# Scores and outputs of a retention head placed between the groups of the large products that follow its projections

## The chip, the cores and the metric

The kernel runs on one core of one Trainium2 chip. The metric is the device time of one execution in microseconds (us), less is better. Engine names in the profile: PE is TensorE (PEld its weight loads), DVE is VectorE, ACT is ScalarE, POOL is GpSimd, SP is SyncE.

## The reference

One decoder layer with two head groups that read the same projected input: 16 RWKV-7 heads of 64 and 4 RetNet heads of 256, for 256 tokens of width 2048. The outputs of both are concatenated and go through one output projection, then a layer norm, an MLP of width 8192 and a second norm. The change is in the RetNet part. Cut down:

```python
def _retention_mix(q, k, v, g, gn_w):
    ...
    q = _rotary(q, cos, sin)
    k = _rotary(k, cos, sin) * RET_HEAD ** -0.5
    ...
    scores = jnp.einsum('bhncd,bhnmd->bhncm', qc, kc) * decay_mask[:, None]
    intra = jnp.einsum('bhncm,bhnme->bhnce', scores, vc)
    ...   # plus the state carried over from the chunk before
    y = _head_norm(y, RET_GN_EPS) * gn_w.reshape(RET_HEADS, RET_HEAD)
    return y.reshape(B, T, D_RET) * jax.nn.silu(g.astype(jnp.float32))
```

Since 256 tokens are two chunks of 128, the kernel computes each head as one masked product over all 256 tokens: the decay between any two tokens is in a mask.

## The kernel before

All weights come as a stream of 202 chunks of 128 x 2048. Each chunk is loaded in two halves into `raw` (three buffers); ScalarE rounds a half to `whi` (L136) and VectorE subtracts for the rest `wlo` (L138), four buffers each. Every large product is three products: high by high, high by low, low by high. A chunk is used in one of two ways. `stat_tile` (L141) keeps the weights as the stationary operand: 48 products of 128x256 at L154. `mov_chunk` (L159) moves them: 24 products of 128x512 at L170. Both yield four times per chunk.

Up to about 480 us the generator `large` issues the input projections of the RWKV units and of the heads. The four RWKV units (each with four heads) are generators of their own with hundreds of small steps: a decay product (L530, L562), a triangular solve on VectorE (`prod` L677, `xb` L680) whose result comes back by DMA and is multiplied at L726, a scan over chunks (L758 to L792, with `rhs` and `sa` copied by ScalarE at L763 and L768), and a norm whose result is written to `mxh` and `mxl` (L816, L817). `interleave` advances each live unit by one step per yield of `large`. A yield of "end" advances no unit; it only counts towards RET_SPLIT, which says after how many of them the next unit's input projections come. The order written out this way is then the input of a scheduler, which may move instructions on each engine.

`retention` (L397) runs twice, for two heads each. It first forms v for both heads (`vt`), four moved chunks. Then for each head and for q and k in turn it issues two `stat_tile`, VectorE multiplies the bank by cosine and sine (`ra` L417, `rb` L419) and GpSimd subtracts and adds the halves into `qk` (L422, L423). After two bare yields come the scores: four products (L434, L436) into a small bank `sc` of a ring of four, two multiplications with the mask by VectorE (`pm`, L439, L440); then "end", and the outputs: three products (L445 to L447), statistics, an inverse root on VectorE and the norm into `vt` (L458). After both heads the gate follows: four moved chunks, a tanh, products with `vt`, and transposes of `gth` at L473.

Of the kernel before, what the change touches and what calls it, by code (L numbers as in the profile page):

```python
# [17 lines left out]
P = 128  # L18
T = 256
# [57 lines left out]
WO_LAST = 58 + 12  # L77

LAG = dict(lora=2, scan=3, sq=5, rn=1, kk=7, bt=2, g1=1, btok=1, ktok=2, g2=1, sub=3, xt=2, vtok=8, bg=4, d1=3, d2=1, f1=1, sa=2, st=2, yc=2)

SUB_YIELD = (6, 10, 13, 16, 19, 21, 23, 25, 27, 29)
NSHORT = 10
# [18 lines left out]
def tile_hybrid_layer(ctx, tc, xT, xtok, ws, pp, lup, glup, ln1r, ln2r, cst, rope, dmask, eye, out):  # L101
# [169 lines left out]
    with ExitStack() as rctx:  # L271
# [124 lines left out]

        def retention():  # L397

            for n in range(2):

                vt = rp.tile([P, 1024], F32, name="vt", tag="vt", bufs=1).rearrange("q (a n) -> q a n", a=2)
                banks = [mm_bank(), mm_bank()]
                for kq in range(4):
                    yield from mov_chunk(tok_act(xh, xl, kq), banks, kq == 0, kq == 3)
                    if kq == 3:
                        for tt in range(2):
                            S.copy(vt[:, tt], banks[tt])
                    yield "end"
                for h in (2 * n, 2 * n + 1):
                    qk = []  # L410
                    for w in range(2):
                        bank = mm_bank()
                        yield from stat_tile(xact, bank[:, hs[0]])
                        yield "end"
                        yield from stat_tile(xact, bank[:, hs[1]])
                        ra, rb_ = tmp("ra"), tmp("rb")
                        V.tensor_tensor(out=ra, in0=bank, in1=ropet, op=ALU.mult)  # L417
                        for i in range(2):
                            V.tensor_tensor(out=rb_[:, hs[i]], in0=bank[:, hs[i]], in1=ropet[:, hs[1 - i]],  # L419
                                            op=ALU.mult)  # L420
                        o = tmp("qk%d" % w)
                        G.tensor_tensor(out=o[:, hs[0]], in0=ra[:, hs[0]], in1=ra[:, hs[1]], op=ALU.subtract)  # L422
                        G.tensor_tensor(out=o[:, hs[1]], in0=rb_[:, hs[0]], in1=rb_[:, hs[1]], op=ALU.add)  # L423
                        qk.append(o)
                        if w == 0:
                            yield "end"
                    q, k = qk
                    yield
                    yield
                    sc = sm_bank()  # L430
                    dmt = rp.tile([P, T], F32, name="dmt", tag="dmt", bufs=2)
                    nc.gpsimd.dma_start(out=dmt, in_=dmask[:, T * h:T * h + T])
                    for i in range(2):
                        TE.matmul(sc[:, 0:T], k[:, T * i:T * i + P], q[:, hs[i]], start=i == 0, stop=i == 1)  # L434
                    for i in range(2):
                        TE.matmul(sc[:, T:T + P], k[:, T * i + P:T * i + T], q[:, T * i + P:T * i + T],  # L436
                                  start=i == 0, stop=i == 1)
                    pm = tmp("pm", n=384)
                    V.tensor_tensor(out=pm[:, 0:T], in0=sc[:, 0:T], in1=dmt, op=ALU.mult)  # L439
                    V.tensor_tensor(out=pm[:, T:T + P], in0=sc[:, T:T + P], in1=dmt[:, 0:P],  # L440
                                    op=ALU.mult)
                    yield "end"
                    yb = sm_bank()
                    hv = slice(T * (h % 2), T * (h % 2) + T)
                    TE.matmul(yb[:, 0:T], pm[:, 0:P], vt[:, 0, hv], start=True, stop=True)  # L445
                    TE.matmul(yb[:, T:2 * T], pm[:, P:T], vt[:, 0, hv], start=True, stop=False)
                    TE.matmul(yb[:, T:2 * T], pm[:, T:T + P], vt[:, 1, hv], start=False, stop=True)  # L447
                    st6 = tmp("st6", n=12)
                    mv = tmp("mv", n=4)
                    for tt in range(2):  # L450
                        V.bn_stats(out=st6[:, 6 * tt:6 * tt + 6], in_=yb[:, hs[tt]])
                        V.bn_aggr(out=mv[:, 2 * tt:2 * tt + 2], in_=st6[:, 6 * tt:6 * tt + 6])
                    var = tmp("rvar", n=2)
                    V.tensor_scalar(out=var, in0=mv.rearrange("q (a b) -> q a b", b=2)[:, :, 1], scalar1=RET_EPS,
                                    scalar2=None, op0=ALU.add)
                    rs = rsqrt(rp, var, 2)
                    for tt in range(2):
                        V.tensor_scalar(out=vt[:, tt, hv], in0=yb[:, hs[tt]], scalar1=mv[:, 2 * tt:2 * tt + 1],  # L458
                                        scalar2=rs[:, tt:tt + 1], op0=ALU.subtract, op1=ALU.mult)

                banks = [mm_bank(), mm_bank()]
                for kq in range(4):
                    yield from mov_chunk(tok_act(xh, xl, kq), banks, kq == 0, kq == 3)
# [690 lines left out]
```

## Time and profile before

| what | value |
|---|---|
| device time, median of 3 runs | 1284.11 us (1282.04 to 1285.03) |
| the profiled execution's own time | 1282.36 us |
| its span in the trace | 1280.6 us |
| PE busy in the span | 1233.7 us, 96% |
| DVE busy | 853.1 us, 67% |
| ACT busy | 560.0 us, 44% |
| POOL busy | 117.3 us, 9% |

The page counts an engine as busy while one of its instructions runs. The chain of work that ended last goes 75% of the span over PE and 11% over DVE; its largest lines are the large products, L170 and L154, with 33% each. A timeline row names the start, the duration, the instruction and, in brackets, how long the engine stood idle before it and what released it. A row of stretches gives each engine's busy time in the stretch and the clock that TensorE was granted, as a share of full speed.

### The profile page before, as it was taken

The page shows a single profiled execution, that of the slowest core. Times are in us where ns is not written, and L with a number is a line of the kernel's source. Part 1 is how long each engine was busy: PE and PEld are TensorE (multiplying, and loading weights), DVE is VectorE, ACT ScalarE, POOL GpSimd, SP SyncE. Part 2 cuts the span into 40 slices and gives each one's busy share as a digit, 9 for nine tenths or more (in the row PEclk, how much of TensorE's full clock was granted, in tenths as well). Part 3 has the DMA queues.
Part 4 walks back from the last instruction along what each step waited for, and adds up shares of the span by engine and source line. Part 5 has one row for each costly group of instructions (what it writes and reads, how often), then busy time and mean ns, then how long its engine had stood idle before and what let it go on. Part 6 is the DMA issues. An engine that isn't in the chain of part 4 may idle for free.

```text
span 1280.6 us, 21924 instructions
## 1 busy us (share of the span) xinstructions
PE 1233.7 (96%) x8952; PEld 1110.1 (87%) x8952; DVE 853.1 (67%) x1311; ACT 560.0 (44%) x723; POOL 117.3 (9%) x97
## 2 busy tenths in 40 slices
PE   7998989999998999989999999999999999999996
PEld 7988888878897778769988899988999888999885
DVE  6898899899979765685654455545555554555566
ACT  5544335355434343464443344433444433444441
POOL 1100121110102100137300000000000000000001
PEclk9999999999999999999999999999999999999998
DMA  8565345345454437555655555555555555555562
GB/s 287 197 187 157 105 142 168 108 153 176 156 144 148 147 112 252 197 176 193 239 198 198 194 188 190 184 192 190 194 190 190 184 192 192 193 190 186 183 213 98
DMA packets 86185, 229.89 MB, mean 180 GB/s; under 512 B 30530, under 2 KB 30658, under 8 KB 85316
## 3 DMA queue, kind: packets, MB, share of 16 engines
q1 hardware_dynamic: 83924, 219.51, 52.5%
q0 software_dynamic: 1440, 7.87, 1.7%
q8 instruction: 70, 1.15, 0.4%
q10 hardware_dynamic: 720, 1.11, 0.3%
q14 instruction: 31, 0.25, 0.1%
HBM read 224.72 MB, written 3.74 MB: 178 GB/s over the span
## 4 chain that ended last, share of the span: by engine, by line
PE 75%; DVE 11%; ACT 3%; DMA 3%; issue 2%; POOL 1%; DVEq 0%; ACTq 0%; POOLq 0%; SPq 0%
PE mm L170 33%; PE mm L154 33%; PE mm L190 4%; DVE wlo L138 3%; DMA raw<-in_ws_dram 2%; DVE prod L677 2%; DVE xb L680 1%; PE sm L623 1%; ACT whi L136 1%; DMA xt<-dxt 1%; POOL qk L423 1%; ACT wx L136 0%; PE sm L766 0%; ACT sw L653 0%; PE sm L758 0%
## 5 line engine op out<-in xcount | busy, mean ns | idle before, releaser
L138 DVE TENSOR_TENSOR wlo<-raw,whi 128x1024 fp32r<-128x1024 f32 x375 | 466.6, 1245 | 330.4 <-ACT whi L136 319.6
L136 ACT CAST whi<-raw 128x1024 fp32r<-128x1024 f32 x376 | 395.0, 1051 | 548.5 <-PE mm L154 235.3
L154 PE MATMUL mm<-x1h,wlo 128*128 128x256 f32 x960 | 269.9, 281 | 0.0
L154 PE MATMUL mm<-x1l,whi 128*128 128x256 f32 x960 | 269.9, 281 | 0.0
L154 PE MATMUL mm<-x1h,whi 128*128 128x256 f32 x960 | 269.8, 281 | 0.0
L154 PEld LDWEIGHTS mm<-x1h,wlo 128*128 128x128 f32 x960 | 183.6, 191 | 0.0
L154 PE MATMUL mm<-xh,whi 128*128 128x256 f32 x640 | 181.8, 284 | 0.0
L154 PEld LDWEIGHTS mm<-x1h,whi 128*128 128x128 f32 x960 | 181.1, 189 | 0.1
L154 PEld LDWEIGHTS mm<-x1l,whi 128*128 128x128 f32 x960 | 180.2, 188 | 0.2
L154 PE MATMUL mm<-xl,whi 128*128 128x256 f32 x640 | 179.9, 281 | 0.0
L154 PE MATMUL mm<-xh,wlo 128*128 128x256 f32 x640 | 179.8, 281 | 0.0
L170 PE MATMUL mm<-whi,ul 128*128 128x512 f32 x448 | 174.3, 389 | 0.0
L170 PE MATMUL mm<-whi,uh 128*128 128x512 f32 x448 | 174.3, 389 | 0.0
L170 PE MATMUL mm<-wlo,uh 128*128 128x512 f32 x448 | 174.3, 389 | 0.0
L154 PEld LDWEIGHTS mm<-xh,whi 128*128 128x128 f32 x640 | 121.5, 190 | 2.9 <-issue 0.9
L154 PEld LDWEIGHTS mm<-xl,whi 128*128 128x128 f32 x640 | 121.5, 190 | 0.9 <-issue 0.2
L154 PEld LDWEIGHTS mm<-xh,wlo 128*128 128x128 f32 x640 | 121.6, 190 | 0.7
L170 PEld LDWEIGHTS mm<-whi,ul 128*128 128x128 f32 x448 | 84.1, 188 | 17.5
L170 PEld LDWEIGHTS mm<-whi,uh 128*128 128x128 f32 x448 | 84.1, 188 | 17.5
L170 PEld LDWEIGHTS mm<-wlo,uh 128*128 128x128 f32 x448 | 84.1, 188 | 17.1
L1044 POOL TENSOR_TENSOR z<-z,lnr 128x512 f32<-128x512 f32 x3 | 3.9, 1292 | 603.0 <-DVE stats L1032 603.0
L170 PE MATMUL mm<-whi,xh 128*128 128x512 f32 x128 | 51.7, 404 | 0.0
(270 smaller groups left out, 1612.5 us busy)
## 6 DMA issues: line engine op xcount, KB each, us to landing
raw<-in_ws_dram SPq DMA_DIRECT2D x400, 512.0 KB, 4.5
first<-in_ws_dram SPq DMA_DIRECT2D x8, 256.0 KB, 8.2
z<-in_xtok_dram POOLq DMA_DIRECT2D x2, 1024.0 KB, 10.8
lnr<-in_ln1r_dram POOLq DMA_DIRECT2D x2, 1024.0 KB, 5.5
lnr<-in_ln2r_dram POOLq DMA_DIRECT2D x2, 1024.0 KB, 11.2
xraw<-in_xT_dram SPq DMA_DIRECT2D x3, 512.0 KB, 8.8
dn<-g SPq DMA_DIRECT2D x8, 128.0 KB, 3.6
xt<-dxt SPq DMA_DIRECT2D x8, 128.0 KB, 3.6
```

The costliest lines, as they stand in the source:

```text
L136: S.copy(hi, raw)
L138: E.tensor_tensor(out=lo, in0=raw, in1=hi.bitcast(F32), op=ALU.subtract)
L154: TE.matmul(dst, w[:, c], a, start=n == 0, stop=n == 3 * KT - 1)
L170: TE.matmul(dsts[tt], a, w[:, c], start=first and k4 == 0 and j == 0, stop=last and k4 == 3 and j == 2)
L190: TE.matmul(dst, a, wt[:, o:o + w], start=kq == 0 and k4 == 0 and i == 0, stop=kq == 3 and k4 == 3 and i == 2)
L423: G.tensor_tensor(out=o[:, hs[1]], in0=rb_[:, hs[0]], in1=rb_[:, hs[1]], op=ALU.add)
L623: TE.matmul(bank[r, 128 * n:128 * n + 128], src[r, c64(p, n)], ar[r, o:o + 128], start=True, stop=True)
L677: V.tensor_tensor(out=pv, in0=xbv[0:q, 0:m, 0:t], in1=blk.rearrange("q (s t) -> q t s", t=32)[0:q, t:t + 1, 0:t].broadcast_to([q, m, t]), ...
L680: V.tensor_reduce(out=xbv[0:q, 0:m, t], in_=pv, axis=AX.X, op=ALU.add)
L1044: G.tensor_tensor(out=z[:, tt, cb(n)], in0=z[:, tt, cb(n)], in1=lnr2[:, 0, cb(n)], op=ALU.mult)
```

## The change

The scores and the outputs of a head become functions of their own. Where the scores stood there is now only a note: `later(4, ...)`. The wrapper `going` around the large products that follow counts their yields and calls a noted function when its count is used up. So the scores are issued after four yields of the next `stat_tile` or `mov_chunk`, which is one chunk, and the outputs four yields after that. The two bare yields ahead of the scores are gone; each "end" stays. The load of the mask `dmt` stays at the head's end. What is computed is the same.

```diff
+RLAG = (4, 4)
...
+            pend = []
+            def later(n, fn):
+                pend.append([n, fn])
+            def going(gen):
+                for m in gen:
+                    yield m
+                    for e in list(pend):
+                        e[0] -= 1
+                        if e[0] <= 0:
+                            pend.remove(e)
+                            e[1]()
+            def scores(h, vt, q, k, dmt):
+                sc = sm_bank()
+                for i in range(2):
+                    TE.matmul(sc[:, 0:T], k[:, T * i:T * i + P], q[:, hs[i]], start=i == 0, stop=i == 1)
...
+                pm = tmp("pm", n=384)
+                V.tensor_tensor(out=pm[:, 0:T], in0=sc[:, 0:T], in1=dmt, op=ALU.mult)
...
+                later(RLAG[1], lambda: outputs(h, vt, pm))
+            def outputs(h, vt, pm):
+                yb = sm_bank()
...
-                    yield from mov_chunk(tok_act(xh, xl, kq), banks, kq == 0, kq == 3)
+                    yield from going(mov_chunk(tok_act(xh, xl, kq), banks, kq == 0, kq == 3))
...
-                        yield from stat_tile(xact, bank[:, hs[0]])
+                        yield from going(stat_tile(xact, bank[:, hs[0]]))
...
-                    q, k = qk
-                    yield
-                    yield
-                    sc = sm_bank()
                     dmt = rp.tile([P, T], F32, name="dmt", tag="dmt", bufs=2)
                     nc.gpsimd.dma_start(out=dmt, in_=dmask[:, T * h:T * h + T])
...
+                    later(RLAG[0], lambda h=h, vt=vt, qk=qk, dmt=dmt: scores(h, vt, *qk, dmt))
                     yield "end"
```

In the kernel after, every line from here on has another number: L154 becomes L156, L170 becomes L172, the scores L434 and L436 become L419 and L421, `pm` L424 and L425, the outputs L431 to L433, and the solve and the scan stand 19 lines later.

TensorE, head 0: the large products (`mm`, from the input's high and low part `xh`, `xl`) around the score products (`sm<-qk`). Before:

```order
L154 MATMUL mm<-xl,whi 128x256
L154 MATMUL mm<-xh,wlo 128x256
L434 MATMUL sm<-qk_1881,qk_2088 128x256
L154 MATMUL mm<-xh,whi 128x256
L154 MATMUL mm<-xl,whi 128x256
L154 MATMUL mm<-xh,wlo 128x256
L154 MATMUL mm<-xh,whi 128x256
L434 MATMUL sm<-qk_1881,qk_2088 128x256
L436 MATMUL sm<-qk_1881,qk_2088 128x128 x2
L154 MATMUL mm<-xl,whi 128x256
```

After, 30 large products later:

```order
L156 MATMUL mm<-xl,whi 128x256
L156 MATMUL mm<-xh,wlo 128x256
L419 MATMUL sm<-qk_1881,qk_2088 128x256 x2
L421 MATMUL sm<-qk_1881,qk_2088 128x128 x2
L156 MATMUL mm<-xh,whi 128x256
```

The four score products moved behind 30 more large products and stand together.

VectorE, head 0: the steps of a unit in its solve (`prod`, `xb`), a subtraction for a weight half (`wlo`), the end of a unit (`mxl`) and the masked scores (`pm`). Before:

```order
L677 TENSOR_TENSOR prod<-xb,blk 96x88
L439 TENSOR_TENSOR pm<-sm,dmt 128x256
L680 TENSOR_REDUCE xb<-prod 96x8
L440 TENSOR_TENSOR pm<-sm,dmt 128x128
L677 TENSOR_TENSOR prod<-xb,blk 96x96
L817 TENSOR_TENSOR mxl<-yt,mxh 128x512
L680 TENSOR_REDUCE xb<-prod 96x8
L138 TENSOR_TENSOR wlo<-raw,whi 128x1024
```

After:

```order
L696 TENSOR_TENSOR prod<-xb,blk 96x88
L140 TENSOR_TENSOR wlo<-raw,whi 128x1024
L699 TENSOR_REDUCE xb<-prod 96x8
L836 TENSOR_TENSOR mxl<-yt,mxh 128x512
L696 TENSOR_TENSOR prod<-xb,blk 96x96
L424 TENSOR_TENSOR pm<-sm,dmt 128x256
L699 TENSOR_REDUCE xb<-prod 96x8
L425 TENSOR_TENSOR pm<-sm,dmt 128x128
```

The masked scores moved behind the subtraction and behind `mxl`.

TensorE, the scan at the end of unit 3, third of its steps: the right sides (`sm<-rhs,xt`), products with the values (`vtok`), with the solution (`sa`) and the large products of the output projection (`mm`, from `mxh`, `mxl`). Before:

```order
L791 MATMUL sm<-st,ar 64x64
L170 MATMUL mm<-whi,mxl 128x512
L170 MATMUL mm<-wlo,mxh 128x512
L766 MATMUL sm<-rhs,xt 64x64 x4
L774 MATMUL sm<-vtok,ktok 64x64
L758 MATMUL sm<-vtok,g_4251 64x64
L170 MATMUL mm<-whi,mxh 128x512
L170 MATMUL mm<-whi,mxl 128x512
L170 MATMUL mm<-wlo,mxh 128x512
L775 MATMUL sm<-sa,btok 64x64
```

After:

```order
L810 MATMUL sm<-st,ar 64x64
L172 MATMUL mm<-wlo,mxh 128x512
L172 MATMUL mm<-whi,mxh 128x512
L785 MATMUL sm<-rhs,xt 64x64 x4
L793 MATMUL sm<-vtok,ktok 64x64
L777 MATMUL sm<-vtok,g_4251 64x64
L172 MATMUL mm<-whi,mxl 128x512
L794 MATMUL sm<-sa,btok 64x64
```

Between the right sides and the first use of `sa` there stands one large product, where there were three.

## Rows read from the trace of the kernel before

**Rows 1.** Busy time of each engine and granted clock up to 480 us.

```profile
core 0: us, PE busy (x) PEld busy (x) DVE busy (x) ACT busy (x) POOL busy (x), PEclk, DMA share, GB/s
0.00:480.00 480.00, 451.34 (x4073) 405.14 (x4074) 402.94 (x851) 221.88 (x350) 57.99 (x63) 0.99 0.51 159
```

**Rows 2.** TensorE's timeline at the score products, heads 0 to 3.

```profile
start us, us, engine line op out<-in xcount [idle before <-releaser]
171.65 0.70 PE L434 MATMUL sm<-qk,qk 128*128 128x256 f32 x2 [1.25 <-POOL qk L422]
...
174.77 0.79 PE L434 MATMUL sm<-qk,qk 128*128 128x256 f32 x1 [1.96 <-POOL qk L423]
...
259.55 0.48 PE L434 MATMUL sm<-qk,qk 128*128 128x256 f32 x1 [0.61 <-POOL qk L423]
...
387.21 0.48 PE L434 MATMUL sm<-qk,qk 128*128 128x256 f32 x1 [0.75 <-POOL qk L422]
...
390.44 0.48 PE L434 MATMUL sm<-qk,qk 128*128 128x256 f32 x1 [1.93 <-POOL qk L423]
...
416.35 0.56 PE L434 MATMUL sm<-qk,qk 128*128 128x256 f32 x1 [2.46 <-POOL qk L422]
...
418.90 0.79 PE L434 MATMUL sm<-qk,qk 128*128 128x256 f32 x1 [0.28 <-POOL qk L423]
```

**Rows 3.** Busy time and granted clock in five short stretches around waits.

```profile
174.00:178.00 4.00, 3.23 (x14) 3.05 (x15) 2.50 (x8) 0.90 (x1) 0.72 (x1) 0.57 0.39 131
...
201.50:205.50 4.00, 3.67 (x17) 3.48 (x18) 4.00 (x9) 3.21 (x5) 1.00 (x2) 0.57 0.21 62
...
390.00:394.00 4.00, 3.49 (x22) 3.14 (x23) 4.00 (x9) 2.93 (x6) 0.38 (x1) 1.00 0.11 29
...
416.30:422.00 5.70, 5.37 (x19) 3.97 (x20) 3.59 (x9) 0.00 (x0) 2.11 (x1) 0.70 0.34 121
...
418.90:421.90 3.00, 3.00 (x13) 2.60 (x14) 1.22 (x4) 0.00 (x0) 0.00 (x0) 0.81 0.51 175
```

**Rows 4.** Busy time around head 0 and around heads 2 and 3.

```profile
155.00:200.00 45.00, 41.18 (x352) 39.54 (x351) 42.11 (x117) 20.58 (x33) 10.17 (x9) 0.96 0.49 147
...
370.00:420.00 50.00, 44.50 (x341) 41.84 (x341) 47.90 (x128) 20.58 (x29) 11.35 (x8) 0.97 0.44 146
```

**Rows 5.** Two stretches full of 128x256 and of 128x512 products.

```profile
160.00:170.00 10.00, 10.00 (x88) 10.00 (x89) 9.52 (x37) 3.69 (x4) 1.26 (x1) 1.00 0.39 123
...
290.00:300.00 10.00, 10.00 (x46) 8.28 (x47) 9.86 (x19) 5.20 (x10) 0.00 (x0) 1.00 0.44 147
```

**Rows 6.** Waits, 160 to 185 us: waited for, total, times, longest.

```profile
PEld sm L445 <- DVE pm L439: 0.3, 1, 0.3
```

**Rows 7.** GpSimd's timeline, the addition of a half of qk.

```profile
172.15 2.57 POOL L423 TENSOR_TENSOR qk<-rb 128x256 f32<-128x256 f32 x1 [0.55 <-DVE rb L419]
...
389.65 0.73 POOL L423 TENSOR_TENSOR qk<-rb 128x256 f32<-128x256 f32 x1 [2.49 <-DVE rb L419]
...
405.57 3.45 POOL L423 TENSOR_TENSOR qk<-rb 128x256 f32<-128x256 f32 x1 [2.43 <-DVE rb L419]
...
416.74 2.11 POOL L423 TENSOR_TENSOR qk<-rb 128x256 f32<-128x256 f32 x1 [0.44 <-DVE rb L419]
```

**Rows 8.** TensorE's timeline at the waits of units and gate.

```profile
201.82 0.80 PE L562 MATMUL sm<-hi,ones 128*128 128x512 f32 x1 [2.44 <-ACT hi L558]
...
224.43 0.24 PE L726 MATMUL sm<-xx,g 32*32 32x32 f32 x2 [0.90 <-DVE xx L715]
...
284.59 0.30 PE L473 MATMUL sm<-c,gth 128*128 128x128 f32 x1 [1.28 <-issue]
```

**Rows 9.** VectorE's timeline near the heads.

```profile
176.94 0.42 DVE L439 TENSOR_TENSOR pm<-sm,dmt 128x256 f32<-128x256 f32 x1 [1.45 <-issue]
...
178.70 0.69 DVE L817 TENSOR_TENSOR mxl<-yt,mxh 128x512 fp32r<-128x512 f32 x1 [0.75 <-ACT mxh L816]
...
405.66 1.20 DVE L138 TENSOR_TENSOR wlo<-raw,whi 128x1024 fp32r<-128x1024 f32 x1
...
414.59 0.67 DVE L417 TENSOR_TENSOR ra<-mm,ropet 128x512 f32<-128x512 f32 x1
```

**Rows 10.** ScalarE's timeline, a copy in unit 3's scan.

```profile
453.52 0.27 ACT L768 COPY sa<-sm 128x128 f32<-128x128 f32 x1 [0.68 <-PE sm L766]
```

More of the change, by code (lines that the diff above doesn't have):

```diff
@@ L397, in retention @@
         def retention():
+            pend = []
[13 more added lines that the diff above has]
+                    TE.matmul(sc[:, 0:T], k[:, T * i:T * i + P], q[:, hs[i]], start=i == 0, stop=i == 1)
+                for i in range(2):
+                    TE.matmul(sc[:, T:T + P], k[:, T * i + P:T * i + T], q[:, T * i + P:T * i + T],
+                              start=i == 0, stop=i == 1)
+                pm = tmp("pm", n=384)
+                V.tensor_tensor(out=pm[:, 0:T], in0=sc[:, 0:T], in1=dmt, op=ALU.mult)
+                V.tensor_tensor(out=pm[:, T:T + P], in0=sc[:, T:T + P], in1=dmt[:, 0:P], op=ALU.mult)
+                later(RLAG[1], lambda: outputs(h, vt, pm))
+            def outputs(h, vt, pm):
+                yb = sm_bank()
+                hv = slice(T * (h % 2), T * (h % 2) + T)
+                TE.matmul(yb[:, 0:T], pm[:, 0:P], vt[:, 0, hv], start=True, stop=True)
+                TE.matmul(yb[:, T:2 * T], pm[:, P:T], vt[:, 0, hv], start=True, stop=False)
+                TE.matmul(yb[:, T:2 * T], pm[:, T:T + P], vt[:, 1, hv], start=False, stop=True)
+                st6 = tmp("st6", n=12)
+                mv = tmp("mv", n=4)
+                for tt in range(2):
+                    V.bn_stats(out=st6[:, 6 * tt:6 * tt + 6], in_=yb[:, hs[tt]])
+                    V.bn_aggr(out=mv[:, 2 * tt:2 * tt + 2], in_=st6[:, 6 * tt:6 * tt + 6])
+                var = tmp("rvar", n=2)
+                V.tensor_scalar(out=var, in0=mv.rearrange("q (a b) -> q a b", b=2)[:, :, 1], scalar1=RET_EPS,
+                                scalar2=None, op0=ALU.add)
+                rs = rsqrt(rp, var, 2)
+                for tt in range(2):
+                    V.tensor_scalar(out=vt[:, tt, hv], in0=yb[:, hs[tt]], scalar1=mv[:, 2 * tt:2 * tt + 1],
+                                    scalar2=rs[:, tt:tt + 1], op0=ALU.subtract, op1=ALU.mult)
             for n in range(2):
@@ L412, in retention @@
                         bank = mm_bank()
-                        yield from stat_tile(xact, bank[:, hs[0]])
+                        yield from going(stat_tile(xact, bank[:, hs[0]]))
                         yield "end"
-                        yield from stat_tile(xact, bank[:, hs[1]])
+                        yield from going(stat_tile(xact, bank[:, hs[1]]))
                         ra, rb_ = tmp("ra"), tmp("rb")
@@ L426, in retention @@
                             yield "end"
-                    q, k = qk
-                    yield
-                    yield
-                    sc = sm_bank()
                     dmt = rp.tile([P, T], F32, name="dmt", tag="dmt", bufs=2)
                     nc.gpsimd.dma_start(out=dmt, in_=dmask[:, T * h:T * h + T])
[L433 to L441, printed above, removed]
-                    yield "end"
-                    yb = sm_bank()
-                    hv = slice(T * (h % 2), T * (h % 2) + T)
-                    TE.matmul(yb[:, 0:T], pm[:, 0:P], vt[:, 0, hv], start=True, stop=True)
@@ L446, in retention @@
[L446 to L459, printed above, removed]
+                    later(RLAG[0], lambda h=h, vt=vt, qk=qk, dmt=dmt: scores(h, vt, *qk, dmt))
@@ L461, in retention @@
+                    yield "end"
                 banks = [mm_bank(), mm_bank()]
                 for kq in range(4):
-                    yield from mov_chunk(tok_act(xh, xl, kq), banks, kq == 0, kq == 3)
+                    yield from going(mov_chunk(tok_act(xh, xl, kq), banks, kq == 0, kq == 3))
                     if kq < 3:
```

## Prediction

> **What bounds the kernel now.** Start with the busy shares of the stretches: the four retention heads lie in the first 480 us, in which TensorE is busy for 451.3 [rows 1]. Its holes there, 28.7 us by that row, are all that this change can reach. Next read TensorE's timeline at the scores. All seven rows say that the product waited for `qk`, the rotated query or key that GpSimd adds up last: 1.25 + 1.96 at head 0, 0.61 at head 1, 0.75 + 1.93 at head 2, 2.46 + 0.28 at head 3, together 9.24 us [rows 2]. So the scores do stand too early. Then read the granted clock beside the waits: after those of head 0 TensorE was busy for 3.23 us of 4 at 0.57 of its clock, near the lower of its two levels (1.2 and 2.4 GHz); at full clock that work takes 3.23 x 0.43 = 1.4 us less. Around head 3 it was 5.37 us at 0.70, 1.6 us lost, of which 3.00 us at 0.81, 0.57 us, lie behind the last score [rows 3]. Last, look at who else is full: VectorE is busy for 42.1 of 45 us around head 0 and for 47.9 of 50 around heads 2 and 3 [rows 4]. There TensorE's waits are partly VectorE's time, and a hole that closes in one place can open at the next.
>
> The prices of the filler are 10.00 us for 88 products of 128x256 and 10.00 us for 46 of 128x512: 0.1136 and 0.217 us each [rows 5].
>
> **What the change moves.** No instruction on the engines is added or removed; the mask's load keeps its place in GpSimd's queue. Counted in the order of the instructions, the scores come 30 products later at head 0 (128x256), 21 at head 1 (128x512), 23 at head 2 and 17 at head 3 (mostly 128x512). Two bare `yield`s per head go, so the units get eight steps fewer.
>
> Outputs: before they already stood 18, 4, 11 and 4 products behind their scores, and at head 0 they waited 0.3 us for `pm` [rows 6]. Putting 48 or 24 products there is worth nothing. The later head norm is needed only by the gate, whose 96 products (96 x 0.217 = 20.8 us) come first. The score and output banks are held longer in a ring of four; I price that at nothing, with the 0.3 as the nearest row, and a bound of 1 us.
>
> Head 0: 30 x 0.1136 = 3.4 us of products now stand ahead. Without its first wait TensorE stood at the score at 171.65 - 1.25 = 170.4, so it comes at 173.8; k's second half was ready at 172.15 + 2.57 = 174.7 [rows 7]. A wait of 0.9 is left of 3.21, too little, I take it, for the clock to fall. Gain 2.3 + 1.4 = 3.7 us.
>
> What survives of it: the next two waits are unit 1's. The first, 2.44 us for `hi` at 201.8 and the half-clock stretch behind it (3.67 us at 0.57, 1.6 us lost) [rows 3, 8], follows a chain that begins with a TensorE product, so it moves along. The second, 0.90 us for `xx` at 224.4 [rows 8], stands behind unit 1's triangular solve, which runs on the nearly full VectorE. VectorE gets earlier only by what it idled itself: 1.45 us before `pm`, since it waited there for the scores, and 0.75 us before `mxl` [rows 9], together 2.20 us. So TensorE arrives 3.7 us early and is released 2.2 us early; its wait grows from 0.90 to 2.4. The single waits of 2.44 and 2.46 us have half clock around them, as have 1.25 and 1.96 together; 0.75 and 1.93 at head 2 left the clock at 1.00 [rows 3]. 2.4 is nearest to the first two, so I charge one more half-clock stretch, 1.6 us: 2.2 - 1.6 = **0.6 us** survives. The bounds are 0.6 and 3.7.
>
> Head 1: the wait of 0.61 us goes (21 x 0.217 = 4.6 us ahead of it), and the gate's transposes, which waited 1.28 us [rows 8], stand 8 products (1.7 us) later. 1.9, less 0.1 for a rest: **1.8 us**. Bounds: 0.6 and 1.9.
>
> Heads 2 and 3 must be taken together. At head 2, 18 more products are done when the key's second half comes (23, less those that already stood between the halves): 18 x 0.1136 = 2.0 us. But head 3's key hangs on `ra` at 414.59, on the full VectorE [rows 4, 9], so it does not come earlier by head 2's gain. When GpSimd ends it at 416.74 + 2.11 = 418.85 [rows 7], 14 more products are done than before (17 later, less the 3 between the halves): 14 x 0.217 = 3.0 us for both heads. TensorE now comes to head 3's scores at 416.35 - 2.46 + 17 x 0.217 - 2.0 = 415.6, waits 0.7 us for the key's first half (there at 416.3) and, behind one product, some 2.25 for the second. That lies between the 0.75 and 1.93 that left the clock and the 1.25 and 1.96 that lowered it. The longer of the two is the nearer to 2.44, so I take a fall: 1.6 us lost behind the scores where 0.57 are lost now, 1.0 more. 3.0 - 1.0 = **2.0 us** for both. Bounds: no fall, 3.0 + 0.57 = 3.6; VectorE follows TensorE after all, 5.4 + 1.6 = 7.0; the fall and no gain from head 2, 2.0 - 2.0 = 0.
>
> Unit 3's end: its last part, from the solve's products on, stands 24 products later, and from there to the unit's end 43 large products are mixed in, not 63. In a scan step one product instead of three now lies between the right sides and the use of `sa`; ScalarE waited 0.68 us for the product ahead of `sa` and copied for 0.27 us [rows 10]. The copy is longer than the one product (0.217) and needs a hand-over at both ends: an estimate of 0.12 us a step, for four steps **-0.5 us**. Bounds: 0, and a wait as long as ScalarE's 0.68 in each of the four, -2.7 us.
>
> Sum: 0.6 + 1.8 + 2.0 - 0.5 = 3.9 us. The profiled execution took 1282.36 us, 1.75 below the median of 1284.11. 1282.36 - 3.9 = 1278.46, and with the 1.75 added back **1280.2 us**. With the terms' likely ends (the full cost at unit 3's end, a gain of 1.7; or neither of the two falls of the clock and no cost at unit 3's end, 3.9 + 1.6 + 1.6 + 0.5 = 7.6) the forecast's own range is 1276.5 to 1282.4.
>
> **A rule against it.** The same 128x256 addition on GpSimd took 0.73 us at 389.65, 2.57 at 172.15, 2.11 at 416.74 and 3.45 at 405.57 [rows 7]; the longest ran beside a `wlo` subtraction of VectorE, which reads two SBUF tiles [rows 9]. The change puts `wlo` ahead of `pm` on VectorE, so those subtractions can now fall on the key's addition. The Trainium skill, "SBUF — State Buffer", section "SBUF: two separate sides", says that GpSimd and a VectorE instruction with two SBUF inputs share a port pair as an exclusive lock, and that the later one is fully blocked. The spread of the rows agrees. Where the lengths stay as they were the forecast holds; where the subtraction comes first, that is rival 1.
>
> **The rivals.**
> 1. *GpSimd's addition gets longer.* It decides at head 3, where k's second half is the release and nothing behind it takes the delay up: 3.45 - 2.11 = 1.3 us later. (At head 0 the wait for `xx` swallows it.) For it: the rows above. Against: 0.73 was seen as well. Gain 3.9 - 1.3 = 2.6: 1281.5 us.
> 2. *All of it is recovered.* The units follow TensorE, and no wait grows: 9.24 + 1.4 + 1.6 = 12.2 us, 1271.9 us. For it: after 201.8 the chain begins with a TensorE product. Against: VectorE's 47.9 of 50 us.
> 3. *The next waits take it back.* VectorE bounds the stretch, and of all that TensorE saves only VectorE's own saving, 2.2 - 1.6 = 0.6 us, stays; nothing of heads 1 to 3: 1283.5 us. For it: VectorE is also nearly full where the heads' own waits are. Against: its rest between heads, and head 1's two waits, which no VectorE work follows closely.
> 4. *Slower: unit 3's end loses its cover.* 20 products fewer, 20 x 0.217 = 4.3 us, become waits, and three of them bring a half-clock stretch of 1.6 each: 9.1 us against the 4.4 gained before: 4.7 slower, 1288.8 us. It decides from 4.4 us of new waits there on. For it: the scan is a chain of small products and copies over three engines. Against: ScalarE and VectorE are freer there, and each step keeps some products.
> That the change does not do what it says is already half true, of the outputs; of the scores the order shows that they moved.
>
> **How the numbers follow.** The forecast 0.48, rival 1 0.10, rival 2 0.13, rival 3 0.19, rival 4 0.10. The predicted time is the forecast's, 1280.2 us. For 8 in 10 the range leaves out rival 4, the slow edge of rival 3 (0.04) and the fast half of rival 2 (0.06): 1271.5 to 1284.0. A measurement of this kernel can tell about 0.2%, 2.6 us, from no change, so faster ends at 1281.5 and slower begins at 1286.7. Faster: 0.39 of the forecast, half of rival 1 (0.05), rival 2 and 0.02 of rival 3, 0.59. Same: the forecast's slow end, 0.09, the other half of rival 1, rival 3's 0.17 and 0.01 of rival 4, 0.32. Slower: 0.09.
>
> **What would show it.** Right: in the timeline after, one score wait of about 0.9 us at head 0 with the clock at 1.00 behind it, none at head 1, 0.7 and 2.2 us at head 3 with half clock behind them, the wait for `xx` near 2.4 us, VectorE without its idle 1.45 before `pm`. Rival 1 shows as additions of 3 us or more ahead of the scores, rival 2 as a wait for `xx` that stays near 0.9, rival 3 as new or longer waits that sum to what the scores lost, rival 4 as waits of TensorE for `sa` or `rhs` in the last scan, with a clock below 1.00. Wrong from the ground up I would be if the scores still waited for `qk` as long as now.

## The result and the profile after

The changed kernel took 1278.28 us (median of 11 runs, 1273.66 to 1286.51), the kernel before 1285.03 (11 runs beside them). The ratio is 0.9939, with a 95% interval of 0.9915 to 0.9963. The same program was timed twice more among the experiments, 0.9970 (0.9952 to 0.9989) and 0.9936 (0.9913 to 0.9959). So it is faster by 0.3 to 0.6%, 4 to 8 us, where 3.9 us were forecast: the three timings lie between about the forecast and twice of it. Its first profiled execution took 1278.70 us with a span of 1276.9, 3.7 below the span before. That this is near 3.9 is chance: head 0's first rotation (the first `ra` row of VectorE) came 2.3 us later, from there to the output projection's first residual (the first row `z<-z,mm` of VectorE) it took 2.7 us less, and behind that, where nothing was changed, 3.3 us less.

The shares of the page hardly show this. After, the page's first part:

```profile
PE 1231.0 (96%) x8952; PEld 1107.3 (87%) x8952; DVE 855.4 (67%) x1311; ACT 560.6 (44%) x723; POOL 118.4 (9%) x97
```

and the stretch that holds the four heads, the same view as [rows 1] (columns as there):

```profile
0.00:480.00 480.00, 451.29 (x4073) 404.79 (x4074) 402.80 (x851) 222.40 (x350) 57.09 (x61) 0.99 0.51 160
```

TensorE is again idle for 28.7 us of these 480, to a tenth. The stretch now holds a little more of the work, and one hole that the change does not touch was larger: unit 0's wait for `xx`, ahead of all the heads, which the timelines before and after show so:

```profile
127.24 0.24 PE L726 MATMUL sm<-xx,g 32*32 32x32 f32 x2 [1.53 <-DVE xx L715]
```

```profile
126.69 0.31 PE L745 MATMUL sm<-xx,g 32*32 32x32 f32 x2 [2.93 <-DVE xx L734]
```

2.93 us and not 1.53, with about half clock behind it, though the order of the instructions up to there is the same. The stretch behind this wait before, after, and in a second trace of the changed kernel, where the wait was 1.78 us:

```profile
126.00:134.00 8.00, 6.76 (x105) 5.72 (x105) 5.24 (x11) 3.50 (x7) 1.70 (x3) 1.00 0.59 200
```

```profile
126.00:134.00 8.00, 7.31 (x61) 6.24 (x61) 3.24 (x6) 2.92 (x5) 1.70 (x3) 0.57 0.48 165
```

```profile
130.00:142.00 12.00, 12.00 (x105) 10.01 (x100) 5.94 (x9) 3.92 (x8) 3.58 (x4) 0.50 0.18 60
```

From `xx` to head 0's first rotation it took 30.8 us before, 33.7 after and 36.5 in the second trace, by chance: 5.7 us, as much as the whole change gains. What the change does must therefore be read from one mark to the next, not from the span's start. These are TensorE's score waits after, the same view as [rows 2]:

```profile
177.13 0.48 PE L419 MATMUL sm<-qk,qk 128*128 128x256 f32 x1 [0.61 <-POOL qk L471]
...
390.81 0.48 PE L419 MATMUL sm<-qk,qk 128*128 128x256 f32 x1 [0.96 <-POOL qk L471]
...
416.57 0.48 PE L419 MATMUL sm<-qk,qk 128*128 128x256 f32 x1 [1.18 <-POOL qk L470]
...
419.35 0.48 PE L419 MATMUL sm<-qk,qk 128*128 128x256 f32 x1 [2.07 <-POOL qk L471]
```

9.24 us in seven waits became 4.82 in four: 0.61 at head 0, none at head 1, 0.96 at head 2, 1.18 + 2.07 at head 3. The three waits that [rows 8] show of before are these after:

```profile
201.67 0.80 PE L581 MATMUL sm<-hi,ones 128*128 128x512 f32 x1 [4.26 <-ACT hi L577]
...
224.82 0.24 PE L745 MATMUL sm<-xx,g 32*32 32x32 f32 x2 [1.19 <-DVE xx L734]
...
286.77 0.30 PE L492 MATMUL sm<-c,gth 128*128 128x128 f32 x1 [1.65 <-issue]
```

The wait for `hi` grew from 2.44 to 4.26 us, that for `xx` from 0.90 to 1.19, that of the gate's transposes from 1.28 to 1.65. So 2.5 us of the 4.4 that the scores lost came back in three other places. The granted clock around the waits, as in [rows 3] (last but two in each row):

```profile
174.00:178.00 4.00, 3.39 (x27) 2.93 (x26) 4.00 (x10) 2.45 (x5) 2.59 (x1) 1.00 0.29 84
...
201.50:205.50 4.00, 3.83 (x16) 3.47 (x17) 4.00 (x9) 3.05 (x5) 0.92 (x2) 0.57 0.39 122
...
224.50:232.00 7.50, 6.74 (x104) 5.63 (x105) 4.98 (x11) 3.40 (x7) 1.70 (x3) 1.00 0.52 179
...
418.00:422.00 4.00, 2.65 (x10) 2.31 (x11) 3.90 (x6) 1.05 (x1) 1.29 (x1) 0.77 0.38 133
...
422.00:426.00 4.00, 4.00 (x15) 3.20 (x15) 2.00 (x4) 0.00 (x0) 0.00 (x0) 0.81 0.65 173
```

Behind head 0 it is at 1.00 where it was at 0.57; behind `hi` it is low as before; behind `xx` it stays up; behind head 3 it is low for about as long as before.

### The profile page after: what moved, and what is told of

Its sections match the earlier page's. It is cut to its first block, busy times and chain, and to the rows that moved or that the text cites. A ratio compares the mean times of both kernels' runs of the same rounds, so it can differ in the third digit from the quotient of the medians.

```text
span 1276.9 us, 21924 instructions
## 1 busy us (share of the span) xinstructions
PE 1231.0 (96%) x8952; PEld 1107.3 (87%) x8952; DVE 855.4 (67%) x1311; ACT 560.6 (44%) x723; POOL 118.4 (9%) x97
## 4 chain that ended last, share of the span: by engine, by line
PE 75%; DVE 11%; DMA 4%; ACT 3%; issue 2%; POOL 0%; DVEq 0%; ACTq 0%; SPq 0%
PE mm L172 34%; PE mm L156 33%; DVE wlo L140 3%; PE mm L192 3%; DMA raw<-in_ws_dram 2%; DVE prod L696 2%; PE sm L642 1%; DMA xt<-dxt 1%; DVE xb L699 1%; ACT whi L138 1%; ACT wx L138 0%; PE sm L785 0%; ACT sw L672 0%; DVE wx L140 0%; PE sm L777 0%
## 5 line engine op out<-in xcount | busy, mean ns | idle before, releaser
L156 PE MATMUL mm<-x1h,wlo 128*128 128x256 f32 x960 | 268.9, 280 | 0.0
L156 PE MATMUL mm<-x1h,whi 128*128 128x256 f32 x960 | 268.8, 280 | 0.0
L156 PE MATMUL mm<-x1l,whi 128*128 128x256 f32 x960 | 268.8, 280 | 0.0
L156 PEld LDWEIGHTS mm<-x1h,wlo 128*128 128x128 f32 x960 | 183.5, 191 | 0.0
L156 PE MATMUL mm<-xh,whi 128*128 128x256 f32 x640 | 182.0, 284 | 0.0
L156 PEld LDWEIGHTS mm<-x1l,whi 128*128 128x128 f32 x960 | 180.2, 188 | 0.2
L156 PEld LDWEIGHTS mm<-x1h,whi 128*128 128x128 f32 x960 | 180.2, 188 | 0.1
L156 PE MATMUL mm<-xh,wlo 128*128 128x256 f32 x640 | 179.3, 280 | 0.0
L156 PE MATMUL mm<-xl,whi 128*128 128x256 f32 x640 | 179.3, 280 | 0.0
L172 PE MATMUL mm<-whi,uh 128*128 128x512 f32 x448 | 174.3, 389 | 0.0
L172 PE MATMUL mm<-whi,ul 128*128 128x512 f32 x448 | 174.3, 389 | 0.0
L172 PE MATMUL mm<-wlo,uh 128*128 128x512 f32 x448 | 174.3, 389 | 0.0
L156 PEld LDWEIGHTS mm<-xh,whi 128*128 128x128 f32 x640 | 121.3, 190 | 2.9 <-issue 0.9
L156 PEld LDWEIGHTS mm<-xl,whi 128*128 128x128 f32 x640 | 121.5, 190 | 0.9 <-issue 0.2
L156 PEld LDWEIGHTS mm<-xh,wlo 128*128 128x128 f32 x640 | 121.3, 189 | 0.6
L172 PEld LDWEIGHTS mm<-wlo,uh 128*128 128x128 f32 x448 | 84.1, 188 | 17.6
L172 PEld LDWEIGHTS mm<-whi,ul 128*128 128x128 f32 x448 | 84.1, 188 | 17.3
L172 PEld LDWEIGHTS mm<-whi,uh 128*128 128x128 f32 x448 | 84.1, 188 | 17.2
L172 PE MATMUL mm<-whi,xh 128*128 128x512 f32 x128 | 52.6, 411 | 0.0
```

The lines of the kernel that those rows point to most:

```text
L156: TE.matmul(dst, w[:, c], a, start=n == 0, stop=n == 3 * KT - 1)
L172: TE.matmul(dsts[tt], a, w[:, c], start=first and k4 == 0 and j == 0, stop=last and k4 == 3 and j == 2)
```

## The experiments

Times of single executions scatter by some 0.3%, so parts worth 2 us are told apart by marks in the traces as well. The marks are starts of rows in the timelines: head 0's first rotation (`ra`), unit 1's `xx` on TensorE, the last rotation of head 1, the first of head 2, and the first residual of the output projection (`z`). In the experiments RLAG holds a pair for each head, yields up to the scores and from there to the outputs; None stands for the old place, with its two bare yields.

**One part alone.** Head 0 alone:

```diff
-RLAG = (4, 4)
+RLAG = ((4, 4), (None, None), (None, None), (None, None))
```

> Only head 0 changed, heads 1 to 3 as before. Theory (VectorE gives it back at unit 1): the scores of head 0 wait about 0.6 us and not 3.2, with the clock at 1.00; the wait for `hi` behind them grows from 2.4 to about 4.3 us; from head 0's first rotation to unit 1's second decay product the stretch is 1 to 2 us shorter than before, and so is the time. Rival (the units move along with TensorE): the wait for `hi` stays at 2.4 us and the time is 3.7 us or more below before.

Measured: 0.9969 (0.9940 to 0.9998). Its timeline on TensorE:

```profile
181.86 0.48 PE L419 MATMUL sm<-qk,qk 128*128 128x256 f32 x1 [0.61 <-POOL qk L473]
...
205.82 0.79 PE L595 MATMUL sm<-hi,ones 128*128 128x512 f32 x1 [3.69 <-ACT hi L591]
```

The score wait is 0.61 us, and `hi` waits 3.69, not 2.44: part of the gain goes into it, as the theory says. The stretch from head 0's first rotation to this product is 40.7 us where it was 43.8, 3.0 shorter and not 1 to 2. The gain is not settled by the time alone (0.3 to 7.7 us); up to `xx` the marks give 66.4 us before and 64.6 here, 1.8.

Head 1 alone:

```diff
+RLAG = ((None, None), (4, 4), (None, None), (None, None))
```

> Only head 1 changed, the others as before. The prediction put 1.8 us there. Theory after the first traces (the norm of head 1, now later, holds the gate's transposes): the score wait of 0.61 us goes, the transposes still wait about 1.6 us, the stretch from head 1's last rotation to head 2's first is 0.5 to 0.9 us shorter than before (116.8 us), and the time is within 2 us of before. Rival (the prediction's step): both waits go, 1.8 us in that stretch.

Measured: 1.0006 (0.9981 to 1.0030). The score wait is gone, the transposes wait 1.65 us, and from head 1's last rotation to head 2's first it is 115.9 us against 116.8: 0.8, as the theory said, and half of the prediction's 1.8.

Heads 2 and 3 alone:

```diff
+RLAG = ((None, None), (None, None), (4, 4), (4, 4))
```

> Only heads 2 and 3 changed, heads 0 and 1 as before. Theory: the score waits there go from 5.4 to about 4.2 us, head 3's rotation comes no earlier, the products behind it run 2 to 4 us earlier, and the time is 2 to 4 us below before, the larger part of the whole change's gain. Rival (heads 0 and 1 carry the gain): the time of before within 1 us.

Measured: 0.9966 (0.9942 to 0.9989), 4.4 us. The three parts, -0.31, +0.06 and -0.34%, add up to the -0.6% of two of the three timings of the whole, though each is known to some 0.25% only. The score waits at heads 2 and 3 were 0.97, 1.32 and 2.05 us, those of the changed kernel, but behind them the clock did not fall:

```profile
418.00:422.00 4.00, 0.79 (x3) 0.30 (x2) 4.00 (x8) 1.94 (x2) 2.56 (x2) 1.00 0.36 133
...
422.00:426.00 4.00, 3.83 (x19) 3.28 (x20) 3.90 (x6) 0.15 (x1) 0.11 (x1) 1.00 0.45 139
```

Outputs alone:

```diff
+RLAG = ((None, 8), (None, 8), (None, 8), (None, 8))
```

> Scores in the old place (both bare yields kept), only the outputs at the place that they have after the change, eight yields behind the head's end. Theory (outputs are worth nothing): the score waits are those of before, 9.2 us together, and the time is that of before, at worst 1.5 us longer by the late norm at head 1's gate. Rival (moving the norm off the crowded stretch is half of the gain): 3 us or more below before.

Measured: 0.9998 (0.9973 to 1.0022). Nothing, as forecast. The gate's transposes behind head 1 now wait longest of all:

```profile
294.06 0.30 PE L506 MATMUL sm<-c,gth 128*128 128x128 f32 x1 [2.80 <-issue]
```

so the late norm does cost there. The rival's 3 us are left only at the edge of the interval (3.5 us).

The two bare yields alone (the kernel before without them):

```diff
-                    yield
-                    yield
```

> The kernel before with one part of the change alone: the two bare yields ahead of the scores are left out in all heads, so the units get eight steps fewer, and scores and outputs stay at the head's end. Theory (the steps are worth nothing by themselves): score waits of 9 to 11 us in all and the time of before within 2 us. Rival (the eight steps, which keep unit work out of VectorE's crowded stretches, are part of the gain): 3 us or more below before.

Measured: 1.0051 (1.0027 to 1.0075), 6.6 us **slower**. Neither theory nor rival had this. The stretch from head 1 to head 2 takes 122.8 us, 6.0 more than before; in it unit 2 waits for `xx` on TensorE, twice, and the clock falls:

```profile
326.67 0.24 PE L756 MATMUL sm<-xx,g 32*32 32x32 f32 x2 [1.33 <-DVE xx L745]
...
328.77 0.32 PE L756 MATMUL sm<-xx,g 32*32 32x32 f32 x4 [1.53 <-DVE xx L745]
```

```profile
326.00:332.00 6.00, 3.80 (x43) 3.49 (x44) 4.39 (x7) 2.92 (x5) 0.00 (x0) 0.67 0.52 173
...
332.00:340.00 8.00, 8.00 (x86) 7.55 (x85) 4.46 (x7) 2.11 (x3) 2.91 (x4) 0.82 0.32 112
```

The waits are 2.9 us, and the clock costs 3.80 x 0.33 = 1.3 and 8.00 x 0.18 = 1.4 us: 5.6 of the 6.0.

Before, no such wait is there. Unit 2's solve runs a step per yield, and its result goes out by DMA (`dxt<-xb`) and comes back as `xt`. SyncE's timeline shows the last sending, before, after the change, and here:

```profile
310.37 0.42 SPq L687 DMA_DIRECT2D dxt<-xb  x1
```

```profile
313.40 0.33 SPq L706 DMA_DIRECT2D dxt<-xb  x1
```

```profile
319.10 0.42 SPq L717 DMA_DIRECT2D dxt<-xb  x1
```

Against a decay product of unit 2 (`mxh,lsp`), which starts on TensorE at 306.50, 307.12 and 310.36, that is 3.9, 6.3 and 8.7 us behind. Fewer yields make the solve end later; before, the margin took it; at 8.7 us it no longer does. In the changed kernel the solve is late too, but TensorE does not wait there. Why its solve loses only 2.4 us with the same number of yields is open: the later places of `pm` and the norm are the likely reason, but the change with the bare yields kept was not tried.

**Where VectorE gives it back.** Outputs right behind the scores:

```diff
-RLAG = (4, 4)
+RLAG = ((4, 1), (4, 1), (4, 1), (4, 1))
```

> The changed kernel with one edit: the outputs are issued one yield after the scores and not four, in all heads. In the trace after the change the gate's transposes behind head 1 still wait 1.65 us, for a product with `vt` that VectorE does right behind the end of head 1's late norm. Theory (the later outputs cost there, the later scores gain): that wait falls below 0.5 us, the score waits stay as after the change (0.6 at head 0, about 1 + 3.2 at heads 2 and 3), and the time is 1 to 2 us below the changed kernel's. Rival (the order of the norm costs nothing, VectorE is full there in any case): the wait stays near 1.65 us and the time is the changed kernel's within 1 us.

Measured: 0.9926 (0.9901 to 0.9951), not to be told from the changed kernel, which was not timed beside it. The transposes' first wait fell to 0.64 us, but their second, which had been 0.2, became 1.34, and three outputs now wait for `pm`:

```profile
182.74 0.48 PE L433 MATMUL sm<-vt,pm 128*128 128x256 f32 x1 [0.70 <-DVE pm L424]
...
398.70 0.79 PE L433 MATMUL sm<-vt,pm 128*128 128x256 f32 x1 [2.42 <-DVE pm L424]
...
427.99 0.48 PE L433 MATMUL sm<-vt,pm 128*128 128x256 f32 x1 [1.66 <-DVE pm L424]
```

The score waits did not stay as they were either: at head 3, which TensorE now reaches later, 0.55 us is left of 1.2 + 2.1. So the expectation fell: a norm in time for the gate's first half is paid for elsewhere on the same engine, and the room between scores and outputs, worth nothing in the old place, is needed in the new one at heads 2 and 3.

Without the inverse root (eleven small VectorE instructions per head are left out, the variance stands in for the root):

```diff
-                rs = rsqrt(rp, var, 2)
+                rs = var
```

> The changed kernel without the inverse root of the head norm (the eleven small VectorE instructions per head are left out, the variance stands in for the root), so VectorE has about 2 us less to do per head. Theory (VectorE is the bound behind the heads): the wait for `hi` behind head 0 shrinks from 4.3 to 2.0 to 3.0 us, the gate's transposes behind head 1 wait less than 0.5 us and not 1.65, and the time is 2 to 5 us below the changed kernel. Rival (these waits are for ScalarE or for TensorE's own chain): both waits stay within 0.5 us and the time within 1 us.

Measured: 0.9928 (0.9906 to 0.9950), 5.2 us in the medians below the changed kernel timed beside it (0.9970). Beside the other two timings of the changed kernel, 0.9939 and 0.9936, it is about 1 us, which the intervals do not tell from nothing. The waits are not as the theory said:

```profile
202.28 0.50 PE L595 MATMUL sm<-hi,ones 128*128 128x512 f32 x1 [3.41 <-ACT hi L591]
...
285.04 0.30 PE L506 MATMUL sm<-c,gth 128*128 128x128 f32 x1 [1.54 <-issue]
```

`hi` waits 3.41 us and the transposes 1.54, far from the 2 to 3 and the 0.5 expected. Towards `hi`, on VectorE the norm of head 0 (two `vt` of 0.5 us), which stands behind the scan `cs` in the changed kernel, moved ahead of it and filled the time that was freed; `cs` started 34.3 us behind head 0's first rotation, where the three traces of the changed kernel have 34.8, 34.3 and 34.5. At the gate the freed time does show, but not in the wait. Head 1's norm ends 4.5 us ahead of the transposes,

```profile
280.03 0.54 DVE L446 TENSOR_SCALAR vt<-sm,mv,rvar 128x256 f32<-128x256 f32 x1
```

and from the tanh of the gate to the transposes it takes 4.0 us, where the changed kernel takes 5.9. But the scheduler put the transposes 8 large products earlier, at their place of before, so they wait about as long as ever. From head 0's first rotation to the first residual it takes 327.9 us in this trace and 329.7, 331.6 and 327.3 in those of the changed kernel. So this run shows neither that less work on VectorE is worth time in the whole nor how much of `hi` is VectorE's.

That VectorE is in `hi`'s chain is shown by ScalarE's timeline before and after:

```profile
196.46 0.63 ACT L548 ACTIVATE dc<-cs 128x512 f32<-128x512 f32 x1 [1.53 <-DVE cs L544]
```

```profile
196.40 0.64 ACT L567 ACTIVATE dc<-cs 128x512 f32<-128x512 f32 x1 [3.46 <-DVE cs L563]
```

ScalarE waits for the scan `cs` in both, 1.53 us and then 3.46. TensorE's decay product ran 4.3 us earlier against head 0's first rotation, `cs` only 2.3 (2.9 and 2.6 in the other two traces of the changed kernel). Behind `cs` ScalarE works without a hole up to `hi`, some 5 us, in both.

**More room for the scores.**

```diff
-RLAG = (4, 4)
+RLAG = ((8, 4), (8, 4), (8, 4), (8, 4))
```

> The changed kernel with the scores eight yields behind the head and not four, the outputs four behind them as now. Theory (what is left is VectorE's): the remaining score waits (0.6, 1.0, 1.2 and 2.1 us) go, but the waits for `hi` at unit 1 and for the gate's transposes behind head 1 grow by about as much, the latter to 3 us or more since the norm is still later, and the time is that of the changed kernel within 2 us. Rival (TensorE's waits at the scores are a loss of their own): 4 us or more below the changed kernel.

Measured: 0.9944 (0.9926 to 0.9962), 2.8 us in the medians below the changed kernel timed beside it, with overlapping intervals, and not below the other two timings of it (0.9939 and 0.9936). No score waits any more. New is a wait of 3.15 us for a weight half at head 3:

```profile
200.40 0.80 PE L595 MATMUL sm<-hi,ones 128*128 128x512 f32 x1 [3.60 <-ACT hi L591]
...
420.16 0.50 PE L172 MATMUL mm<-wlo,xh 128*128 128x512 f32 x1 [3.15 <-DVE wlo L140]
```

```profile
420.16:424.16 4.00, 4.00 (x18) 3.31 (x19) 3.94 (x6) 0.00 (x0) 0.00 (x0) 1.00 0.56 175
```

The theory had said that the waits for `hi` and of the transposes would grow; they did not (3.60 and 1.57). The 2.8 us lie between the theory's 2 and the rival's 4, so neither is shown. The 3.15 us is for `wlo` of VectorE, which works without a hole there, so VectorE is what is late next at head 3; the clock stays at 1.00 behind it.

A mixture by these waits, and the same with more room at head 2:

```diff
-RLAG = (4, 4)
+RLAG = ((6, 2), (4, 1), (6, 2), (8, 2))
```

> A mixture by the waits that the earlier runs showed: scores 6, 4, 6 and 8 yields behind heads 0, 1, 2 and 3, outputs 2, 1, 2 and 2 yields behind those. Theory: no score waits at heads 0 to 2 and at most 1 us at head 3, no output waits as with one yield, and head 1's norm early enough for the gate, so 1 to 3 us below the changed kernel. Rival (VectorE gives all of it back at unit 1 and behind head 3): the changed kernel's time within 1 us.

Measured: 0.9942 (0.9924 to 0.9961), 4.1 us in the medians below the changed kernel timed beside it, but not below the other two timings of it (0.9939 and 0.9936). The scores of all heads go without waiting. The outputs of head 2 don't, and the clock falls behind them:

```profile
399.21 0.80 PE L433 MATMUL sm<-vt,pm 128*128 128x256 f32 x1 [3.66 <-DVE pm L424]
```

```profile
400.00:404.00 4.00, 4.00 (x16) 3.55 (x15) 3.97 (x14) 0.00 (x0) 0.88 (x1) 0.50 0.34 121
```

```diff
+RLAG = ((6, 2), (4, 1), (6, 4), (8, 2))
```

> The mixture again with head 2's outputs four yields behind its scores and not two, since they waited 3.66 us for `pm` with half clock behind. Theory: that wait falls below 0.5 us, the clock there stays at 1.00, no score waits, and the time is 2 to 5 us below the mixture's (0.994 of before) and 3 to 7 us below the changed kernel. Rival (VectorE, full there, gives it back at head 3 or at the next weight halves): the mixture's time within 1.5 us, with a new wait of 2 us or more for `wlo` or `qk` near head 3.

Measured: 1273.06 us, 0.9908 (0.9883 to 0.9932), beside 1276.95 and 0.9936 for the changed kernel: 3.9 us in the medians, with overlapping intervals. It is the fastest that was run. The output wait went from 3.66 to 0.71 with the clock at 1.00 behind it, and waits of 1.92 for `wlo` near head 3 and of 0.96 at its outputs came in its place:

```profile
202.93 0.50 PE L595 MATMUL sm<-hi,ones 128*128 128x512 f32 x1 [4.07 <-ACT hi L591]
...
399.98 0.48 PE L433 MATMUL sm<-vt,pm 128*128 128x256 f32 x1 [0.71 <-DVE pm L424]
...
419.49 0.51 PE L172 MATMUL mm<-wlo,xh 128*128 128x512 f32 x1 [1.92 <-DVE wlo L140]
...
428.48 0.48 PE L433 MATMUL sm<-vt,pm 128*128 128x256 f32 x1 [0.96 <-DVE pm L424]
```

The time is as its theory said, and so are the clock and the scores, but 0.71 is not below 0.5, and the rival's new wait is there with 1.92 for 2. A wait of 3.4 to 4.3 us for `hi` stays in every version with the later scores at head 0.

**The changed kernel again**, twice.

> The changed kernel once more, for a second trace of it. Single executions differ by some us in stretches that the change does not touch (unit 0's solve, the layer norm). Theory (the stage sums hold): from head 0's first rotation to unit 1's `hi` 41 to 42 us, as in the first trace, where the trace before has 43.75; score waits 0.6, about 1.0, 1.2 and 2.1 us; time 0.4 to 0.9% below before. Rival (the first trace of the change was chance): that stretch is 43 us or more, or the score waits differ by more than 0.5 us.

> The changed kernel a third time, for its time beside the other runs of this call and a third trace. Expected: 0.3 to 0.6% below before; score waits 0.6, 1.0, 1.2 and 2.1 us, 3.7 to 4.3 us for `hi` at unit 1, 1.65 us at the gate's transposes; a half-clock stretch behind head 3 and behind the wait for `xx` in some of its traces only.

Measured: 0.9970 and 0.9936, as above; the first is a little less than the 0.4 to 0.9% expected. From head 0's first rotation to `hi` it takes 41.3, 40.8 and 41.0 us in the three traces, so the first was not chance. The score waits repeat within 0.2 us, `hi` waits 4.26, 3.76 and 4.01 us, the transposes 1.65 in each. What differs is the clock. Behind the wait for `xx` of 1.33 us the second trace has the half-clock stretch that the first and third lack:

```profile
228.50:236.00 7.50, 6.17 (x66) 5.17 (x67) 3.24 (x6) 2.92 (x5) 1.72 (x3) 0.77 0.60 201
```

6.17 us busy at 0.77: 1.4 us lost. Behind the scores of head 3, with equal waits, all three of these traces have one and that of heads 2 and 3 alone has none. The Trainium skill, "TensorE: Matmul & The Clock Gate", section "Part 1: The HAM clock gate", says that the window in which activity is counted runs freely and does not start with the kernel; no run here shows the window, but equal waits with and without a fall agree with it.

The old order has such a spread too, at head 2. In the trace before the waits of 0.75 and 1.93 us there left the clock at 1.00 [rows 3]. In the four other traces with the scores of head 2 in the old place the same two waits were followed by 0.57 to 0.67, with head 1 alone by 0.64, with head 0 alone so:

```profile
392.82 0.48 PE L419 MATMUL sm<-qk,qk 128*128 128x256 f32 x1 [0.75 <-POOL qk L472]
...
396.04 0.80 PE L419 MATMUL sm<-qk,qk 128*128 128x256 f32 x1 [1.93 <-POOL qk L473]
```

```profile
396.00:400.00 4.00, 3.96 (x19) 3.76 (x20) 3.93 (x9) 2.53 (x6) 0.00 (x0) 0.61 0.23 67
```

That is 1.3 to 1.7 us lost, four times in five. With the scores later, one wait of 0.96 to 0.99 us is left at head 2, and the clock behind it was 1.00 in all four traces, so in the first one after the change:

```profile
390.00:394.00 4.00, 3.19 (x25) 3.14 (x26) 3.85 (x6) 3.92 (x8) 0.72 (x1) 1.00 0.06 14
```

The marks, in us (the kernels with the old order in a stretch against those with the changed one; the second number of the old order in the first two rows is that with the outputs alone moved):

| stretch | old order | changed order | gain of the means | forecast |
|---|---|---|---|---|
| head 0's first rotation to unit 1's `xx` | 66.4, 66.7, 66.9, 66.0 | 64.5, 65.1, 63.4, 64.6 | 2.1 | 2.2 |
| the same to head 1's last rotation | 98.3, 98.6, 98.8, 97.9 | 96.9, 98.5, 95.3, 96.5 | 1.6 | 0.6 |
| to head 2's first rotation | 116.8, 117.1, 116.9 | 116.2, 116.5, 115.5, 115.9 | 0.9 | 1.8 |
| to the output projection's first residual | 117.4, 118.5, 121.2 | 116.6, 116.7, 116.6, 114.6 | 2.9 | 1.5 |

The last three together: 5.4 us, where 3.9 were forecast; the first row is part of the second. From `xx` to head 1's last rotation it takes 31.9 us in all traces of the old order, and 32.4, 33.4, 31.9 and 31.9 in the changed one.

## Why the prediction was right

**The bound** was read rightly: the score waits were in part TensorE's own loss, and VectorE, nearly full, turns part of the gain into new waits. Of the 9.24 us about half went. That the total came out is in part luck: head 1 gained less than forecast, and the stretches before and behind it more.

**Head 0, at the scores:** 0.9 us of wait were forecast with the clock up; 0.61 came, at 1.00. VectorE's idle 1.45 us before `pm` is gone, as the prediction said:

```profile
179.92 0.40 DVE L424 TENSOR_TENSOR pm<-sm,dmt 128x256 f32<-128x256 f32 x1
```

TensorE stood at the wait for `hi` 4.3 us earlier against head 0's first rotation, where 3.7 were forecast.

**What survives of it:** the amount was right, the place was not. "The first [...] follows a chain that begins with a TensorE product, so it moves along" failed: between that product and `hi` stands VectorE's `cs`, and that came 2.3 us earlier. So `hi` took 1.8 us back, and `xx`, forecast at 2.4, waits only 1.2 (1.33 and 0.37 in the other two traces). Up to there 2.1 us survive, and 2.2 was VectorE's own saving in the sum. The further half-clock stretch that the sum charged at 1.6 us came in one trace of three and cost 1.5 there; in the first trace a second wait for `xx` cost 0.5. That is why 1.6 and not 0.6 us is left on average.

**Head 1:** 1.8 us were forecast, 0.9 came. The step that failed is "The later head norm is needed only by the gate, whose 96 products [...] come first", and with it that the 1.28 us of the transposes would go. VectorE's timeline after shows that the norm ends just ahead of the gate's use of `vt`:

```profile
284.90 0.54 DVE L444 TENSOR_SCALAR vt<-sm,mv,rsq_y 128x256 f32<-128x256 f32 x1
...
285.99 0.68 DVE L489 TENSOR_TENSOR gth<-gth,vt 128x512 f32<-128x512 f32 x1
```

The transposes wait for that second row. The 20.8 us of gate products are there, but the outputs stand behind 48 of the 96 and the norm's small steps take the rest between the units' steps. With the norm early, as in the run with the outputs one yield behind the scores, the wait is 0.64.

**Heads 2 and 3:** head 3's last rotation came 41.5 us behind head 2's first in all three traces of the changed kernel, as in the trace before: head 2's gain did not reach the key, as forecast. (With head 0 alone and head 1 alone it came 42.2 and 42.4 us behind; beside these, which lost clock at head 2, the key is 0.7 to 0.9 us earlier.) Waits of 4.2 us are left of 5.42, where 3.6 were forecast, and the clock fell behind them as assumed, in three traces of four. The step that was mis-sized is the clock at head 2: the prediction took it as undisturbed from the one trace that it had, and in four other traces of the old order it fell, 1.3 to 1.7 us that the change saves and the sum has at nothing. That is about what the table has above the forecast, 2.9 us against 1.5. But the old order itself scatters from 117.4 to 121.2, so the size stays open.

**Unit 3's end:** TensorE waits for neither `sa` nor `rhs` there. 0.53 us came, behind the unit's last step:

```profile
479.61 0.50 PE L172 MATMUL mm<-whi,mxl 128*128 128x512 f32 x1 [0.53 <-DVE mxl L836]
```

The price, 0.5, was right by accident; the place was the handing over of `mxl`, not the scan. The 0.12 us a step that it was made of is in no row.

**The bare yields** were priced at nothing without a row. In the change no trace shows a wait for them; alone they cost 6.6 us. What they cost within the change is not shown, since the change was not run with them kept. The step had no ground.

**The rivals.** GpSimd's additions that release the scores took 2.59, 0.72 and 1.94 us, so the first rival did not happen:

```profile
174.48 2.59 POOL L471 TENSOR_TENSOR qk<-rb 128x256 f32<-128x256 f32 x1 [0.57 <-DVE rb L467]
...
390.04 0.72 POOL L471 TENSOR_TENSOR qk<-rb 128x256 f32<-128x256 f32 x1 [2.52 <-DVE rb L467]
...
417.36 1.94 POOL L471 TENSOR_TENSOR qk<-rb 128x256 f32<-128x256 f32 x1 [0.83 <-DVE rb L467]
```

Full recovery (12.2 us) is out by the larger waits for `hi`, the full return (a gain of 0.6 us) by the three timings, the slower case by unit 3's end.

## What to carry to other kernels

When work moves off a wait, ask of the next waits behind it which engine stands last in their chain, not which stands first: here a chain that began on the freed TensorE moved only as far as the fullest engine in it, VectorE. An engine's later work needs a date as well: the outputs had nothing to gain from room, but their norm had a user. And a yield or a slot that only paces other work has a price that its own instructions do not show; take it away alone before calling it nothing. Where a sum hangs on whether the clock falls behind a wait, one trace is not enough: at head 2 the one at hand was the exception.

## What the runs showed of the hardware

Equal waits of TensorE were followed by a low clock in some executions and by full clock in others: 0.75 and 1.93 us at head 2 by 0.57 to 0.67 in four traces and by 1.00 in one, 1.2 to 1.4 and 2.1 us with one product between them at head 3 by about half clock in three traces and by 1.00 in a fourth. A single wait of 1.33 us was followed by a clock of 0.77 over 7.5 us, and one of 3.15 us (for `wlo`, with the scores eight yields behind) by 1.00. One more or less such stretch is worth 1.3 to 1.7 us at the heads; behind unit 0's `xx` it was 2.8 us in one trace and 5.7 in another. With the transfer of unit 0's result, whose wait was between 1.0 and 3.6 us over the traces with one and the same order of instructions, that makes single executions differ by as much as the change moves.
